# A two-layer decoder trunk on one core: the last products cut into columns of 512, 256 and 256, the last row normalised in other steps, and new tables of orders

## The chip, the cores and the metric

One Trainium2 chip; the program runs on one of its cores. Five engines work side by side, each through its own list of instructions: TensorE (PE, matmuls; PEld are its weight loads), VectorE (DVE), ScalarE (ACT), GpSimd (POOL) and SyncE (SP, which here only starts transfers). They wait for one another through semaphores. The metric is the device time of one execution in microseconds (us); lower is better. Before the change three runs gave 552.26, 552.55 and 552.84 us.

## What is computed

Two layers over 256 positions of width 1024, all in float32. Each layer has a token mixer (gated spatial mixing in the first, causal attention in the second) beside cross-attention into 256 memory tokens, one output projection, and a SwiGLU channel mixer. Each of the two sublayers ends in a residual and a layer norm:

```python
sub = jnp.concatenate([mix, mem_out], axis=-1) @ w_mix_out[i]
x = layer_norm(ALPHA * x + sub, ln_mix_g[i], ln_mix_b[i])
x = layer_norm(ALPHA * x + swiglu(x, w_ffn_in[i], w_ffn_out[i]), ln_ffn_g[i], ln_ffn_b[i])
```

The change is in the second of these norms in the last layer, whose result is the output.

## The kernel before

The 256 positions are two row tiles of 128 partitions (tt = 0 and 1; `xres[tt]` holds the residual, 128 x 1024). Every operand of a product is split into a high part, which ScalarE rounds (L379), and a low part, the rest, which VectorE subtracts (L380); each product is then three matmuls (high by high, and the two mixed ones). Weights stream from HBM by SyncE into four raw buffers, are split into ten buffers `spl`, and are used once.

The first stage multiplies the input (`x0T`, transposed) with the weights `v` in eight slices of 128 rows, two slices to a transfer block `raw_v`; then come `hqm`, six products `pu`, `hkm` (memory keys, weights `km0`), `pvm` (memory values, `vm0`) and so on. The channel mixer has eleven chunks of 256 hidden columns, whose products go into the accumulators `fof` in the first layer and `fog` in the second.

The end: for tile 0 the last chunks are added to its accumulators, the residual is formed in two halves (L493, sums for mean and variance at L499), and `finish` normalises and stores it. For tile 1 (`last_tile`), the chunks before the last three are already in the accumulators and are added first (L896); the last three chunks, six terms of 128 rows by three passes, are multiplied in pieces of columns (`LAST_PIECES`: 512, 384, 128), each piece into a PSUM tile `last` of its own by 18 matmuls. After each piece VectorE adds it to the residual (L903) and takes its sums (L499), and at the end `finish` runs for tile 1. `finish` (L502 to L514) aggregates mean and variance `mv` (L505), adds epsilon (L507, on VectorE), raises the result to -0.5 on GpSimd (L508), giving the scale `rs`; then, piece by piece, it subtracts the mean and multiplies by the gain (L511), multiplies by `rs` and adds the offset (L512), and starts the transfer to the output (L514, the last piece by ScalarE's queue, the others by SyncE's). L511 needs only the mean, L512 also the scale.

What sets the order: PE's instructions run as the program is written. For VectorE, ScalarE and SyncE three tables of numbers (`VECTOR_ORDER`, `SCALAR_ORDER`, `SYNC_ORDER`) say in which order the instructions of the engine, counted as written, are put into its list; `keep_order` ties each to the one ahead of it, so that an engine never overtakes a waiting instruction. GpSimd's few instructions are placed by the scheduler.

Of the kernel before, what the change touches and what calls it, by code (L numbers as in the profile page):

```python
# [21 lines left out]
P = 128  # L22
D = 1024
# [6 lines left out]
PIECES = ((0, 512), (512, 1024))  # L30
LAST_PIECES = ((0, 512), (512, 896), (896, 1024))
# [7 lines left out]
EPS = 1e-5  # L39
# [154 lines left out]
class Stream:  # L194
# [128 lines left out]
)  # L323
SCALAR_ORDER = (
# [42 lines left out]
def build(nc, tc, ins, out):  # L367
    ET = mybir.EngineType
    with (
# [115 lines left out]
        class LayerNorm:  # L485
# [16 lines left out]
            def finish(self, gb, store=False):  # L502
                r, tt = self.r, self.tt
# [719 lines left out]
```

## Time and profile before

| | before |
|---|---|
| runs, median (lowest to highest) | 552.55 us (552.26 to 552.84) |
| span of the profiled execution, first to last instruction | 550.8 us |
| clock granted to TensorE, mean | 0.996 |
| HBM read, written | 119.42 MB, 1.05 MB |

The span is that of one execution, taken by the hardware profiler; the runs are timed from outside, and their median lies 1.75 us above the span. In a timeline row stand the start in us from the span's beginning, the duration, the engine, the line, the operation, output and inputs, shapes, the count, and in brackets the idle time of the engine ahead of it and what ended it. In a row of the chain of work that ended last stand start, duration, engine, tile, line and count.

### The profile page before, as it was taken

To read this page: it belongs to the slowest core of one execution; us is meant where nothing else is said; L and a number is where in the kernel's file an instruction comes from. 1 tells how busy PE (TensorE), PEld (TensorE's weight loads), DVE (VectorE), ACT (ScalarE), POOL (GpSimd) and SP (SyncE) were. 2 spreads that over 40 slices of the span, in tenths; PEclk is the share of its full clock that TensorE was granted. 3 is DMA by queue.
4 is the path that set the end of the run, shared out by engine and by line. 5 is a ranking of instruction groups with operands and counts; after the bars stand their busy time and mean duration, and the time that the engine had idled before them with its cause. 6 is when DMAs were issued, how large, how long until landed. Compare 5 with 4: busy or idle time off the path is not lost.

```text
span 550.8 us, 7698 instructions
## 1 busy us (share of the span) xinstructions
PE 542.6 (99%) x2835; PEld 460.6 (84%) x2835; DVE 501.5 (91%) x707; ACT 374.5 (68%) x574; POOL 47.7 (9%) x59
## 2 busy tenths in 40 slices
PE   9999999999999999999999999999999999999994
PEld 8988878888888888888898888788888888888884
DVE  5799978999999999999989688589999999999997
ACT  5868759785858677683565667668768676876720
POOL 1012001020202020100000000111202020201000
PEclk9999999999999999999999999999999999999998
DMA  8997668479796988878539234513597698897622
GB/s 303 384 398 265 223 259 221 154 131 328 155 343 132 300 220 229 275 271 273 198 137 397 105 130 161 114 77 153 97 360 133 249 266 271 233 255 220 218 69 77
DMA packets 23718, 120.97 MB, mean 220 GB/s; under 512 B 2688, under 2 KB 4736, under 8 KB 13824
## 3 DMA queue, kind: packets, MB, share of 16 engines
q1 hardware_dynamic: 17344, 99.16, 47.8%
q0 software_dynamic: 5760, 20.97, 21.4%
q8 instruction: 22, 0.36, 0.3%
q10 hardware_dynamic: 576, 0.34, 0.3%
q14 instruction: 16, 0.13, 0.1%
HBM read 119.42 MB, written 1.05 MB: 219 GB/s over the span
## 4 chain that ended last, share of the span: by engine, by line
PE 98%; DMA 1%; DVE 1%; DVEq 0%; ACT 0%; issue 0%
PE fof L404 11%; PE Xf L404 10%; PE Xg L404 10%; PE fog L404 9%; PE Zg L404 7%; PE Zf L404 7%; PE qk L404 6%; PE opc L404 4%; PE opa L404 4%; PE va L404 3%; PE bv L404 3%; PE pu L404 3%; PE pvm L404 3%; PE hkm L404 2%; PE hqm L404 2%; PE pg L404 2%
## 5 line engine op out<-in xcount | busy, mean ns | idle before, releaser
L379 ACT CAST spl_s_M<-raw_s_T 128x1024 fp32r<-128x1024 f32 x80 | 82.4, 1052 | 22.9 <-DVE raw_s_T L259 18.0
L380 DVE TENSOR_TENSOR spl_s_M<-raw_s_T,spl_s_M 128x1024 fp32r<-128x1024 f32 x80 | 95.6, 1217 | 2.4 <-ACT spl_s_M L379 2.1
L380 DVE TENSOR_TENSOR spl_s_M<-raw_s,spl_s_M 128x1024 fp32r<-128x1024 f32 x60 | 71.7, 1217 | 3.2 <-ACT spl_s_M L379 3.1
L379 ACT CAST spl_s_M<-raw_s 128x1024 fp32r<-128x1024 f32 x60 | 61.0, 1050 | 17.5 <-DMA raw_s<-in_w 13.3
L404 PE MATMUL fof<-spl_w,htf 128*128 128x512 f32 x264 | 63.0, 390 | 0.0
L404 PEld LDWEIGHTS fof<-spl_w,htf 128*128 128x128 f32 x264 | 49.3, 188 | 10.2
L404 PE MATMUL fog<-spl_w,htg 128*128 128x512 f32 x228 | 54.2, 390 | 0.0
L380 DVE TENSOR_TENSOR spl_w<-raw_w,spl_w 128x1024 fp32r<-128x1024 f32 x44 | 53.2, 1215 | 0.1
L404 PEld LDWEIGHTS fog<-spl_w,htg 128*128 128x128 f32 x228 | 42.7, 188 | 8.8
L259 DVE TENSOR_TENSOR raw_s_T<-raw_s_T,raw_s 128x1024 f32<-128x1024 f32 x40 | 48.4, 1217 | 0.1
L379 ACT CAST spl_w<-raw_w 128x1024 fp32r<-128x1024 f32 x44 | 45.7, 1055 | 1.0 <-PE fof L404 1.0
L404 PE MATMUL qk<-x2T,spl_qk 128*128 128x512 f32 x192 | 36.0, 343 | 0.0
L220 POOL DMA_DIRECT2D raw_s<-in_w x20 | 17.1, 856 | 217.1 <-DVE spl_s_M L380 201.4
L404 PEld LDWEIGHTS qk<-x2T,spl_qk 128*128 128x128 f32 x192 | 29.4, 188 | 4.4
L404 PE MATMUL Xg<-spl_s_M,SgM 128*128 128x512 f32 x120 | 29.4, 394 | 0.0
L404 PE MATMUL Xf<-spl_s_M,SfM 128*128 128x512 f32 x120 | 29.3, 393 | 0.0
L404 PE MATMUL Zg<-spl_s_M,SgM 128*128 128x512 f32 x120 | 28.9, 390 | 0.0
L404 PE MATMUL Xf<-spl_s_M,x1T 128*128 128x512 f32 x120 | 28.9, 390 | 0.0
L404 PE MATMUL Zf<-spl_s_M,SfM 128*128 128x512 f32 x120 | 28.8, 389 | 0.0
L404 PE MATMUL Xg<-spl_s_M,x3T 128*128 128x512 f32 x120 | 28.8, 389 | 0.0
L404 PEld LDWEIGHTS Zg<-spl_s_M,SgM 128*128 128x128 f32 x120 | 22.5, 188 | 4.8 <-DVE SgM L380 0.2
L404 PEld LDWEIGHTS Xg<-spl_s_M,x3T 128*128 128x128 f32 x120 | 22.5, 188 | 4.7
(265 smaller groups left out, 1068.8 us busy)
## 6 DMA issues: line engine op xcount, KB each, us to landing
raw_w<-in_w SPq DMA_DIRECT2D x22, 1024.0 KB, 6.6
raw_s<-in_w SPq DMA_DIRECT2D x20, 1024.0 KB, 7.1
raw_s_T<-in_w SPq DMA_DIRECT2D x10, 1024.0 KB, 7.0
raw_s_T<-in_w POOLq DMA_DIRECT2D x20, 512.0 KB, 8.6
raw_s<-in_w POOLq DMA_DIRECT2D x20, 512.0 KB, 5.5
raw_o<-in_w SPq DMA_DIRECT2D x8, 1024.0 KB, 6.4
raw_qk<-in_w SPq DMA_DIRECT2D x6, 1024.0 KB, 4.8
raw_v<-in_w SPq DMA_DIRECT2D x7, 512.0 KB, 8.1
```

Source lines behind the costliest of these rows:

```text
L220: self.nc.gpsimd.dma_start(self.raw[name][:, sl], self.unit_ap(other)[:, sl], accum_op=ALU.add)
L259: self.nc.vector.tensor_add(raw, raw, self.raw[used[1]][:, sl])
L379: nc.scalar.copy(hi, src)
L380: nc.vector.tensor_sub(lo, src, hi.bitcast(F32))
L404: nc.tensor.matmul(o, lhsT, rhs, start=start, stop=stop, skip_group_check=on)
```

## The change

`LAST_PIECES` becomes 512, 256, 256. In `finish`, tile 1 now adds epsilon on GpSimd, subtracts the mean in one step of 1024 columns and scales in two steps of 768 and 256 columns, stored by SyncE and ScalarE; tile 0 goes from three pieces to two of 512, both stored by SyncE. The program's numbering changes with it, and all three tables are replaced as a whole.

```diff
-LAST_PIECES = ((0, 512), (512, 896), (896, 1024))
+LAST_PIECES = ((0, 512), (512, 768), (768, 1024))
+END_PIECES = ((0, 768), (768, 1024))
...
 VECTOR_ORDER = (
-    0, 2, 3, 4, 5, 6, 7, 8, 9, 10, 11, 12, 13, 14, 16, 15, 18, 17, 19, 20, 22, 21, 23, 24, 34, 29, 33, 25, 32, 38, 37,
+    0, 2, 4, 3, 6, 5, 7, 8, 10, 11, 9, 12, 14, 13, 15, 16, 18, 19, 17, 20, 22, 21, 23, 24, 31, 29, 33, 34, 1, 55, 37,
...
                 rs = sm(f"rs{self.nm}{tt}")
-                nc.vector.tensor_scalar_add(rs, mv[:, 1:2], EPS)
+                last = store and tt == 1
+                (nc.gpsimd if last else nc.vector).tensor_scalar_add(rs, mv[:, 1:2], EPS)
                 nc.gpsimd.tensor_tensor(rs, rs, mhalf, ALU.pow)
-                for i, (c0, c1) in enumerate(LAST_PIECES if store else PIECES):
+                for c0, c1 in ((0, D),) if last else PIECES:
                     sl = slice(c0, c1)
                     nc.vector.scalar_tensor_tensor(r[:, sl], r[:, sl], mv[:, 0:1], gb[:, 0, sl], ALU.subtract, ALU.mult)
+                for i, (c0, c1) in enumerate(END_PIECES if last else PIECES):
+                    sl = slice(c0, c1)
                     nc.vector.scalar_tensor_tensor(r[:, sl], r[:, sl], rs, gb[:, 1, sl], ALU.mult, ALU.add)
                     if store:
-                        (nc.scalar if i == len(LAST_PIECES) - 1 else nc.sync).dma_start(out[tt * P:(tt + 1) * P, sl], r[:, sl])
+                        (nc.scalar if last and i else nc.sync).dma_start(out[tt * P:(tt + 1) * P, sl], r[:, sl])
```

Four lines of the file are added ahead of and in this function, so a line of the old numbering stands 1 to 4 lines lower in the new one (L380 is L381, L512 is L516, L903 is L907).

What the change puts where is shown at three places of VectorE's list. The first is the end of the program, from the add of the last piece on. Before:

```order
L903 TENSOR_TENSOR xres<-xres,last_4984 128x128
L499 BN_STATS stg_4939<-xres 128x6
L505 BN_AGGR mvg_5005<-stg_4939 128x2
L511 SCALAR_TENSOR_TENSOR xres<-xres,mvg_5005,gb1ffn 128x128
L507 TENSOR_SCALAR rsg_5007<-mvg_5005 128x1
L511 SCALAR_TENSOR_TENSOR xres<-xres,mvg_5005,gb1ffn 128x384
L511 SCALAR_TENSOR_TENSOR xres<-xres,mvg_5005,gb1ffn 128x512
L512 SCALAR_TENSOR_TENSOR xres<-xres,rsg_5007,gb1ffn 128x128
L512 SCALAR_TENSOR_TENSOR xres<-xres,rsg_5007,gb1ffn 128x384
L512 SCALAR_TENSOR_TENSOR xres<-xres,rsg_5007,gb1ffn 128x512
```

The same place now, with the last scale of tile 0 (`rsg_4927`) ahead of it:

```order
L516 SCALAR_TENSOR_TENSOR xres<-xres,rsg_4927,gb1ffn 128x512
L907 TENSOR_TENSOR xres<-xres,last_4981 128x256
L500 BN_STATS stg_4936<-xres 128x6
L506 BN_AGGR mvg_5002<-stg_4936 128x2
L513 SCALAR_TENSOR_TENSOR xres<-xres,mvg_5002,gb1ffn 128x1024
L516 SCALAR_TENSOR_TENSOR xres<-xres,rsg_5004,gb1ffn 128x768
L516 SCALAR_TENSOR_TENSOR xres<-xres,rsg_5004,gb1ffn 128x256
```

Ten steps became six; epsilon left VectorE and stands on GpSimd ahead of the power there, and the smallest scale, which came first, now comes last.

The second place is the start of the first stage on VectorE: the cast of a slice of `x0T`, its low part, and the low parts of the weight slices (`spl_v0_0` is the first, `spl_v0_1` the second; both halves of the first transfer block `raw_v0`). Before:

```order
L439 CAST x0T_80<-raw_v0_135 128x256
L440 TENSOR_TENSOR x0T_80<-raw_v0_135,x0T_80 128x256
L380 TENSOR_TENSOR spl_v0_0_136<-raw_v0_135,spl_v0_0_136 128x384 x2
L439 CAST x0T_80<-raw_v0_135 128x256
L440 TENSOR_TENSOR x0T_80<-raw_v0_135,x0T_80 128x256
L380 TENSOR_TENSOR spl_v0_1_158<-raw_v0_135,spl_v0_1_158 128x384 x2
```

Now:

```order
L440 CAST x0T_80<-raw_v0_135 128x256
L381 TENSOR_TENSOR spl_v0_0_136<-raw_v0_135,spl_v0_0_136 128x384
L441 TENSOR_TENSOR x0T_80<-raw_v0_135,x0T_80 128x256
L440 CAST x0T_80<-raw_v0_135 128x256
L381 TENSOR_TENSOR spl_v0_0_136<-raw_v0_135,spl_v0_0_136 128x384
L441 TENSOR_TENSOR x0T_80<-raw_v0_135,x0T_80 128x256
L381 TENSOR_TENSOR spl_v0_1_158<-raw_v0_135,spl_v0_1_158 128x384
```

The second low part of the first slice moved behind the cast of the second slice.

The third place is VectorE's stretch ahead of `hkm`, with the low part of the second half of `km0` (`spl_km0_1`). Before:

```order
L965 SCALAR_TENSOR_TENSOR vn_318<-vn_318,mvv0_581,gv_308 128x768
L380 TENSOR_TENSOR memT2_525<-mraw2_314,memT2_525 128x512
L961 BN_AGGR mvv1_588<-stv1_366 128x2
L380 TENSOR_TENSOR spl_km0_1_545<-raw_km0_305,spl_km0_1_545 128x1024
L951 TENSOR_TENSOR uT1_423<-uT1_423,pu11_451 128x256
```

Now:

```order
L970 SCALAR_TENSOR_TENSOR vn_318<-vn_318,rsv0_583,gv_308 128x768
L965 BN_AGGR mvv1_588<-stv1_366 128x2
L955 TENSOR_TENSOR uT1_423<-uT1_423,pu11_451 128x256
L967 TENSOR_SCALAR rsv1_590<-mvv1_588 128x1
L381 TENSOR_TENSOR spl_vm0_0_603<-raw_vm0_391,spl_vm0_0_603 128x1024
L969 SCALAR_TENSOR_TENSOR vn_318<-vn_318,mvv1_588,gv_308 128x768
L381 TENSOR_TENSOR spl_vm0_1_614<-raw_vm0_391,spl_vm0_1_614 128x1024
L381 TENSOR_TENSOR spl_km0_1_545<-raw_km0_305,spl_km0_1_545 128x1024
```

The step moved behind one add of `uT1`, two steps of `vn` and both low parts of `vm0`.

112 rows, old and new, of tables (SCALAR_ORDER, SYNC_ORDER, VECTOR_ORDER) are left out of this document.

## The prediction, made before the changed kernel ran

> **What bounds the kernel now.** I read the page first (busy shares and the clock), then PE's waits, then the chain of work that ended last, then the timeline of the last 16 us.
>
> ```profile
> span 550.8 us, 7698 instructions
> PE 542.6 (99%) x2835; PEld 460.6 (84%) x2835; DVE 501.5 (91%) x707; ACT 374.5 (68%) x574; POOL 47.7 (9%) x59
> PE 98%; DMA 1%; DVE 1%; DVEq 0%; ACT 0%; issue 0%
> PE warmup L415 <- DVE warm L410: 1.1, 1, 1.1
> ```
>
> The first two lines are totals: TensorE (PE) is busy in 99% of the span. The third is the chain that ended last, 98% of it PE. The fourth is the only row in which the list of waits names PE itself as waiting. So the time can change in three ways only: PE gets less work, PE begins to wait, or the stretches before its first and behind its last matmul change.
>
> All durations come from the one profiled execution, with a span of 550.8 us. The median of the runs is 552.55, so 1.75 us lie outside the span; I make the sum against 550.8 and add the same 1.75.
>
> ```profile
> 242.17 2.72 PE Zf L404 x12
> 279.45 9.36 PE bv L404 x54
> 288.81 5.55 PE hqm L404 x32
> 534.57 9.26 PE last L404 x54
> ```
>
> These rows of the chain give the pitch of back-to-back matmuls. 512 columns: 2.72/12 = 0.227 us. 384 columns: 9.36/54 = 0.173. hqm alternates 512 and 256 columns: 5.55/16 = 0.347 a pair, less 0.227 is 0.120 for 256. The last products are 18 of each width, so 128 columns cost (9.26 - 18 x 0.227 - 18 x 0.173)/18 = 0.114, hardly less than 256.
>
> **The last products.** 18 x (0.227 + 0.120 + 0.120) = 8.41 instead of 9.26: **-0.85 us**, all on the bounding engine.
>
> This is where a rule of the Trainium skill speaks against the change: "TensorE: Matmul & The Clock Gate", Back-to-back issue gap, puts a warm matmul at N/2.4 + 2.5 ns, so that 384 + 128 columns cost as much as 256 + 256. By it this term would be nil. The measured 0.114 for 128 columns is twice its 0.056, so I go by the rows.
>
> **Behind the last matmul.** It ends at 534.57 + 9.26 = 543.83; call that E.
>
> ```profile
> 535.35 0.68 DVE L499 BATCH_NORM_STATS2 stg<-xres 128x6 f32<-128x512 f32 x1
> 543.85 0.29 DVE L903 TENSOR_TENSOR xres<-xres,last 128x128 f32<-128x128 f32 x1
> 544.17 0.29 DVE L499 BATCH_NORM_STATS2 stg<-xres 128x6 f32<-128x128 f32 x1
> 544.50 0.24 DVE L505 BATCH_NORM_AGGREGATE mvg<-stg 128x2 f32<-128x18 f32 x1
> 544.77 0.35 DVE L511 SCALAR_TENSOR_TENSOR xres<-xres,mvg,gb1ffn 128x128 f32<-128x128 f32 x1
> 545.04 0.15 DVE L507 TENSOR_SCALAR rsg<-mvg 128x1 f32<-128x1 f32 x1
> 545.11 0.61 DVE L511 SCALAR_TENSOR_TENSOR xres<-xres,mvg,gb1ffn 128x384 f32<-128x384 f32 x1
> 545.27 0.85 POOL L508 TENSOR_TENSOR rsg<-rsg,mhalf 128x1 f32<-128x1 f32 x1 [7.93 <-DVE rsg L507]
> 545.63 0.74 DVE L511 SCALAR_TENSOR_TENSOR xres<-xres,mvg,gb1ffn 128x512 f32<-128x512 f32 x1
> 547.09 0.74 DVE L512 SCALAR_TENSOR_TENSOR xres<-xres,rsg,gb1ffn 128x512 f32<-128x512 f32 x1
> 51.08 0.41 DVE L951 TENSOR_TENSOR uT<-uT,pu 128x256 f32<-128x256 f32 x1
> 51.60 1.02 DVE L966 SCALAR_TENSOR_TENSOR vn<-vn,rsv,gv 128x768 f32<-128x768 f32 x1
> ```
>
> Columns: start, duration, engine, line, instruction. Before, the power on POOL lay beside the subtractions, and DVE never waited: its last step ends at 547.83 = E + 4.00. Now:
>
> - the add and the sums take 256 columns instead of 128: 0.41 (the uT row is an add from PSUM of that width) and about 0.43 (between 0.29 for 128 and 0.68 for 512). With 0.03 between steps and the aggregate's 0.24, the mean is ready at E + 1.19 instead of E + 0.91.
> - one subtraction of 1024 columns. From 0.35 for 128 and 0.74 for 512 follows 1.0 ns a column, so 1.27: E + 1.22 to E + 2.50.
> - beside it POOL now has two steps, epsilon and power. Epsilon on POOL is nowhere in the trace, and what matters is whether POOL may start.
>
> ```profile
> 374.87 1.22 DVE L380 TENSOR_TENSOR spl_s_M<-raw_s_T,spl_s_M 128x1024 fp32r<-128x1024 f32 x1
> 375.04 1.46 POOL L522 TENSOR_TENSOR rsc<-rsc,mhalf 128x1 f32<-128x1 f32 x1 [9.82 <-DVE rsc L521]
> 80.71 0.55 POOL L522 TENSOR_TENSOR rsa<-rsa,mhalf 128x1 f32<-128x1 f32 x1 [29.14 <-DVE rsa L521]
> 80.77 1.23 DVE L380 TENSOR_TENSOR spl_s_M<-raw_s_T,spl_s_M 128x1024 fp32r<-128x1024 f32 x1
> 91.03 0.41 DVE L470 TENSOR_TENSOR kkm<-hkm,kkm 128x256 fp32r<-128x256 f32 x1
> 91.21 0.56 POOL L522 TENSOR_TENSOR rsa<-rsa,mhalf 128x1 f32<-128x1 f32 x1 [3.93 <-DVE rsa L521]
> ```
>
> The same power of 128 x 1 takes 0.55 when it starts ahead of the DVE step (80.71) or beside one that reads PSUM (91.03), and 1.46 when a DVE step with two SBUF operands already runs: it then ends 0.41 behind that step (376.09, 376.50). At 545.27 too: DVE's 384-column step ended at about 545.72, the power at 546.12. The new epsilon waits for the aggregate, as the subtraction does; POOL started 0.08 behind its releaser in the last power, DVE 0.03. So I take it that DVE is first and POOL is held until E + 2.50; then epsilon 0.41, power 0.42, 0.03 to DVE: the scale is there at E + 3.36. DVE, which had this cover before, now **stands idle 0.9 us**. Bounds for the two POOL steps: if nothing holds them and both take the 0.55 of a free power, the scale is ready at E + 2.4, before the subtraction ends; if epsilon costs as much as the slowest power here, 1.46, it comes 1.05 later.
>
> The Trainium skill ("SBUF — State Buffer", SBUF: two separate sides) says that whichever of the two starts first holds the shared ports for its whole instruction. Were POOL first, DVE's subtraction would wait some 0.5 us and the power would queue behind it, about 0.2 us later than my sum. That half isn't seen here: at 80.77 DVE took its usual 1.23 beside a running power.
>
> - the 768-column scale: 1.02 (the vn row): E + 4.38, against E + 4.00 for the last step before. The 256-column one ends at about E + 4.78.
>
> ```profile
> out<-xres SPq DMA_DIRECT2D x2, 256.0 KB, 2.2
> out<-xres SPq DMA_DIRECT2D x2, 192.0 KB, 1.9
> out<-xres ACTq DMA_DIRECT2D x2, 64.0 KB, 1.6
> ```
>
> The last column is issue to landing. 0.3 for each 128 KB more: 384 KB takes 2.35 to 2.8, I take 2.5, that is 0.3 more than the 256 KB that ended the kernel. The 128 KB from ACT (about 1.75) is issued 0.4 later and lands first. So the end moves to **E + 0.38 + 0.30 = 0.68 later behind E**.
>
> Whether DVE is ready at the new E: the first tile's last scale (0.74) stands just ahead of the last add. The pieces now end at 538.7, 540.8 and 542.98. Between 540.8 and 542.98 DVE has an add (0.41), two sums (0.68 and 0.43) and that scale (0.74): 2.26, less the 0.08 by which steps overlap, 2.0. It fits with nothing to spare; no term.
>
> **The start.**
>
> ```profile
> 5.31 17.52 PE va L404 x96
> 5.29 1.07 DVE L380 TENSOR_TENSOR spl_v<-raw_v,spl_v 128x384 fp32r<-128x384 f32 x2
> 7.17 0.29 DVE L439 CAST x0T<-raw_v 128x256 fp32r<-128x256 f32 x1 [0.80 <-DMA raw_v<-in_w]
> 7.42 0.85 PE L404 MATMUL va<-spl_v,x0T 128*128 128x384 f32 x4
> ```
>
> PE needs the second low part of the first weight slice at its eleventh matmul, two behind the 7.42 at which the fourth row begins: 7.42 + 2 x 0.173 = 7.77. Before, it was ready at 6.36. In the new DVE order it stands behind the cast that waits for a DMA until 7.17: 7.17 + 0.29 + 0.55 = 8.01. PE has run without a gap since, so the **0.24 us** stay to the end. No later load lets PE regain it.
>
> **The rest of the tables.** PE's order is the same but for the last 54 matmuls. The step that lost most room is the low part of km0's second half.
>
> ```profile
> 37.86 1.16 DVE L380 TENSOR_TENSOR spl_km<-raw_km,spl_km 128x1024 fp32r<-128x1024 f32 x1
> 45.02 5.55 PE hkm L404 x32
> 30.00:38.00 8.00, 8.00 (x48) 7.06 (x48) 8.00 (x15) 5.22 (x8) 0.00 (x0) 1.00 1.00 411
> ```
>
> The third row is a stretch of 8 us with the busy time of PE, weight loads, DVE, ACT and POOL. The step ended at 39.02, and PE uses it from its ninth matmul on, 45.02 + 4 x 0.347 = 46.41. Ahead of it now stand two adds (0.41 each), two steps of 768 (1.02), two low parts of vm0 (about 1.2) and small ones: 5.6 us, so 44.6 if nothing else is late. 1.8 us of room are left of 7.4. At the other places where I set the work now ahead of a step against the time at which PE needs it, some tenths of a microsecond or more remain; I cost those moves at nothing, covered by the work that PE still has in hand there, with 0 to 1 us as bounds.
>
> **Sum:** -0.85 + 0.68 + 0.24 = +0.07: 550.9 of span, **552.6 us**.
>
> **Rivals.**
>
> 1. POOL isn't held by the subtraction (the epsilon gets through as the power at 80.71 did). For it: only some 0.05 us separate the two starts. Against it: the row at 375.04. DVE's idle 0.9 goes: 551.7, and 551.2 if the 384 KB land as fast as 256 KB and the start keeps its room.
> 2. Slower: DVE reaches km0's second half late. Place: PE at 46.4. It decides once DVE is more than 1.8 us behind; beyond that each microsecond costs one. For it: DVE is busy 8.00 of the 8.00 us between 30 and 38, and in the new ScalarE order two activations that wait for PE's last va matmul (22.83) stand ahead of the casts of u0. With 3.5 us of delay: 552.6 + 1.7 = 554.3.
> 3. 256 columns save nothing over 384 + 128, as the formula has it: the -0.85 falls out, 553.5. Against it: 0.120 is measured in 16 pairs of hqm.
>
> **How the numbers follow.** My forecast, POOL held, no new wait beyond the start, 551.9 to 553.4 with its DMA and epsilon bounds: 0.56. Rival 1: 0.22. Rival 2: 0.17. Rival 3: 0.05. About 0.2%, 1.1 us, is what a measurement of this kernel can tell from no change; so faster is below 551.45, slower above 553.65. Faster: about half of rival 1, 0.11. Slower: rival 2, and a little of the forecast's upper end and of rival 3: 0.19. Same: 0.70. The range runs from rival 1 with a short start to rival 2 at 1.4 us beyond the forecast: 551.3 to 554.0.
>
> **What would show it.** The chain's last-products piece at 8.4 us; POOL's epsilon ending about 0.4 behind the end of the 1024-column subtraction and DVE idle some 0.9 us before the 768-column scale; last DVE step to span end near 3 us; va at 17.7 to 17.8 instead of 17.52. I am wrong on POOL if epsilon ends while the subtraction runs, and on the tables if PE shows a wait of more than 0.3 us anywhere behind the start.

## The result, and the profile after

| | before | after |
|---|---|---|
| runs, median (lowest to highest) | 552.75 us (552.26 to 553.15, 6 runs) | 555.24 us (554.39 to 557.17, 6 runs) |
| ratio after to before | | 1.0051 (95% interval 1.0039 to 1.0063) |
| span of the profiled execution | 550.8 us | 552.7 us |
| last matmul ends | 543.83 | 544.50 |
| from there to the end of the span | 6.97 | 8.20 |

The change made the kernel slower by 2.5 us; 552.6 was predicted, between 551.3 and 554.0. The profiled execution of the changed kernel took 554.39 us, the fastest of its six, so its trace shows the least of the loss, 1.9 us of span. First its totals and the whole list of waits of PE:

```profile
span 552.7 us, 7683 instructions
PE 542.6 (98%) x2835; PEld 459.4 (83%) x2835; DVE 500.4 (91%) x701; ACT 375.0 (68%) x574; POOL 50.4 (9%) x60
PE warmup L416 <- DVE warm L411: 1.0, 1, 1.0
PE hkm L405 <- DVE spl_km L381: 0.8, 1, 0.8
```

PE still bounds, but there is a second row where before had one: hkm waits for the low part of km0. The chain of work that ended last says where else the time went (start, duration, tile, line, count):

```profile
5.17 17.78 PE va L405 x96
34.14 3.03 PE pu L405 x16
47.85 4.34 PE hkm L405 x23
52.19 2.77 PE pvm L405 x16
536.03 8.47 PE last L405 x54
```

The stage va ends at 22.95 instead of 5.31 + 17.52 = 22.83 (+0.12). pvm begins at 52.19 instead of 45.02 + 5.55 = 50.57: +1.50 more, in the stretch in which the chain leaves PE between 37 and 47.85. The last products begin at 536.03 instead of 534.57, so 0.16 was regained in between. They take 8.47 instead of 9.26 (-0.79), and the stretch behind them is 8.20 instead of 6.97 (+1.23). 0.12 + 1.50 - 0.16 - 0.79 + 1.23 = 1.90, the whole of it.

The 1.50 is more than the one wait in the list. PE's and its weight loads' timelines, after and then (last row) before:

```profile
28.34 17.14 PE L405 MATMUL pu<-x0T,spl_u 128*128 128x512 f32 x96
47.85 4.34 PE L405 MATMUL hkm<-memT,spl_km 128*128 128x256 f32 x23 [0.76 <-DVE spl_km L381]
48.45 3.43 PEld L405 LDWEIGHTS hkm<-memT,spl_km 128*128 128x128 f32 x20 [0.19 <-DVE memT L381]
28.22 16.80 PE L404 MATMUL pu<-x0T,spl_u 128*128 128x512 f32 x96
```

The products pu took 0.34 longer, hkm waited 0.76 for km0, and the other 0.40 lie in what is left of hkm behind that wait, where the weight loads wait once more, for a part of memT that VectorE makes after km0's.

The stretch ahead of hkm, in the timeline of VectorE and GpSimd, after and then (last two rows) before:

```profile
42.02 1.22 DVE L381 TENSOR_TENSOR spl_vm<-raw_vm,spl_vm 128x1024 fp32r<-128x1024 f32 x1
43.16 1.01 DVE L969 SCALAR_TENSOR_TENSOR vn<-vn,mvv,gv 128x768 f32<-128x768 f32 x1
44.09 2.58 DVE L381 TENSOR_TENSOR spl_vm<-raw_vm,spl_vm 128x1024 fp32r<-128x1024 f32 x1
46.59 1.21 DVE L381 TENSOR_TENSOR spl_km<-raw_km,spl_km 128x1024 fp32r<-128x1024 f32 x1
43.62 1.97 POOL L933 TENSOR_SCALAR_AFFINE_SELECT wsT<-wsT 128x1536 f32<-128x1536 f32 x1
```

```profile
39.84 1.55 POOL L929 TENSOR_SCALAR_AFFINE_SELECT wsT<-wsT 128x1536 f32<-128x1536 f32 x1 [37.78 <-DMA wsT<-in_wsT]
40.87 1.60 DVE L380 TENSOR_TENSOR spl_vm<-raw_vm,spl_vm 128x1024 fp32r<-128x1024 f32 x1 [0.46 <-ACT spl_vm L379]
```

The reader is to see the 2.58: a step that takes 1.22 elsewhere ended 1.08 after GpSimd's select of wsT did (43.62 + 1.97 = 45.59). The select, which no table lists, was placed behind the second power `rsv` by the scheduler. The same is in the trace of before, in small: 1.60, ended 1.08 behind the select. The prediction had overlooked that row.

The end, in the timelines of VectorE and GpSimd, and the transfers from issue to landing:

```profile
544.52 0.42 DVE L907 TENSOR_TENSOR xres<-xres,last 128x256 f32<-128x256 f32 x1 [0.15 <-PE last L405]
544.98 0.43 DVE L500 BATCH_NORM_STATS2 stg<-xres 128x6 f32<-128x256 f32 x1
545.44 0.24 DVE L506 BATCH_NORM_AGGREGATE mvg<-stg 128x2 f32<-128x18 f32 x1
545.71 1.28 DVE L513 SCALAR_TENSOR_TENSOR xres<-xres,mvg,gb1ffn 128x1024 f32<-128x1024 f32 x1
547.77 1.41 DVE L516 SCALAR_TENSOR_TENSOR xres<-xres,rsg,gb1ffn 128x768 f32<-128x768 f32 x2 [0.77 <-POOL rsg L510]
545.77 1.32 POOL L509 TENSOR_SCALAR rsg<-mvg 128x1 f32<-128x1 f32 x1 [5.96 <-DVE mvg L506]
547.17 0.57 POOL L510 TENSOR_TENSOR rsg<-rsg,mhalf 128x1 f32<-128x1 f32 x1
out<-xres SPq DMA_DIRECT2D x1, 384.0 KB, 2.4
out<-xres ACTq DMA_DIRECT2D x1, 128.0 KB, 2.4
```

Epsilon took 1.32 because the subtraction held it, and VectorE stood idle for 0.77. VectorE's last step ends at 549.18, 4.68 behind the last matmul (before 4.00), and from there to the end it is 3.52 (before 2.97): ScalarE's 128 KB took 2.4 us, as long as the 384 KB of the other queue, and ended the kernel.

### The profile page after: what moved, and what is told of

It reads as the page before. It is cut to its first block, busy times and chain, and to the rows that moved or that the text cites. A ratio compares the mean times of both kernels' runs of the same rounds, so it can differ in the third digit from the quotient of the medians.

```text
span 552.7 us, 7683 instructions
## 1 busy us (share of the span) xinstructions
PE 542.6 (98%) x2835; PEld 459.4 (83%) x2835; DVE 500.4 (91%) x701; ACT 375.0 (68%) x574; POOL 50.4 (9%) x60
## 4 chain that ended last, share of the span: by engine, by line
PE 96%; DVE 2%; ACT 0%; POOL 0%; issue 0%; POOLq 0%; DVEq 0%
PE fof L405 11%; PE Xg L405 10%; PE Xf L405 10%; PE fog L405 9%; PE Zg L405 7%; PE Zf L405 7%; PE qk L405 6%; PE opc L405 4%; PE opa L405 4%; PE va L405 3%; PE bv L405 3%; PE pvm L405 3%; PE hqm L405 2%; PE pg L405 2%; PE pf L405 2%; PE hkm L405 2%
## 5 line engine op out<-in xcount | busy, mean ns | idle before, releaser
L380 ACT CAST spl_s_M<-raw_s_T 128x1024 fp32r<-128x1024 f32 x80 | 82.5, 1051 | 24.9 <-DVE raw_s_T L260 14.0
L381 DVE TENSOR_TENSOR spl_s_M<-raw_s_T,spl_s_M 128x1024 fp32r<-128x1024 f32 x80 | 95.5, 1217 | 2.0 <-ACT spl_s_M L380 1.9
L381 DVE TENSOR_TENSOR spl_s_M<-raw_s,spl_s_M 128x1024 fp32r<-128x1024 f32 x60 | 71.7, 1216 | 2.3 <-ACT spl_s_M L380 2.3
L380 ACT CAST spl_s_M<-raw_s 128x1024 fp32r<-128x1024 f32 x60 | 61.0, 1050 | 14.8 <-DMA raw_s<-in_w 13.3
L405 PE MATMUL fof<-spl_w,htf 128*128 128x512 f32 x264 | 63.0, 390 | 0.0
L405 PEld LDWEIGHTS fof<-spl_w,htf 128*128 128x128 f32 x264 | 49.3, 188 | 10.2
L405 PE MATMUL fog<-spl_w,htg 128*128 128x512 f32 x228 | 54.2, 390 | 0.0
L381 DVE TENSOR_TENSOR spl_w<-raw_w,spl_w 128x1024 fp32r<-128x1024 f32 x44 | 53.1, 1217 | 0.2 <-ACT spl_w L380 0.2
L405 PEld LDWEIGHTS fog<-spl_w,htg 128*128 128x128 f32 x228 | 42.7, 188 | 8.8
L380 ACT CAST spl_w<-raw_w 128x1024 fp32r<-128x1024 f32 x44 | 45.9, 1051 | 1.3 <-ACT spl_w L380 0.8
L405 PE MATMUL qk<-x2T,spl_qk 128*128 128x512 f32 x192 | 36.0, 343 | 0.0
L405 PEld LDWEIGHTS qk<-x2T,spl_qk 128*128 128x128 f32 x192 | 29.4, 188 | 4.4
L405 PE MATMUL Xf<-spl_s_M,SfM 128*128 128x512 f32 x120 | 29.4, 393 | 0.0
L405 PE MATMUL Xg<-spl_s_M,SgM 128*128 128x512 f32 x120 | 29.4, 393 | 0.0
L405 PE MATMUL Xg<-spl_s_M,x3T 128*128 128x512 f32 x120 | 29.1, 390 | 0.0
L405 PE MATMUL Xf<-spl_s_M,x1T 128*128 128x512 f32 x120 | 28.9, 389 | 0.0
L405 PE MATMUL Zf<-spl_s_M,SfM 128*128 128x512 f32 x120 | 28.8, 389 | 0.0
L405 PE MATMUL Zg<-spl_s_M,SgM 128*128 128x512 f32 x120 | 28.8, 389 | 0.0
L221 POOL DMA_DIRECT2D raw_s_T<-in_w x20 | 17.5, 877 | 121.9 <-DVE mix L381 69.7
L405 PEld LDWEIGHTS Xg<-spl_s_M,x3T 128*128 128x128 f32 x120 | 22.4, 188 | 5.0 <-DVE x3T L381 0.4
```

The source lines that it names most:

```text
L221: self.nc.gpsimd.dma_start(self.raw[name][:, sl], self.unit_ap(other)[:, sl], accum_op=ALU.add)
L380: nc.scalar.copy(hi, src)
L381: nc.vector.tensor_sub(lo, src, hi.bitcast(F32))
L405: nc.tensor.matmul(o, lhsT, rhs, start=start, stop=stop, skip_group_check=on)
```

## The experiments

Three theories stood against each other. Theory 1: the loss ahead of the last products is the wait at hkm, made by the select. Theory 2: it belongs to the tables as a whole, at several places. Theory 3: it belongs to the changed end. Each was timed beside runs of the kernel before on the same chip, in groups on five chips; whether the chip adds to the spread between versions isn't shown. "new" and "old" are the tables after and before, the old ones with the numbers of the new program.

| version | ratio to before (interval) | profiled span |
|---|---|---|
| again: after, once more | 1.0060 (1.0047 to 1.0073) | 552.6 |
| end_alone: old tables, new end | 1.0005 (0.9997 to 1.0014) | 551.0 |
| tables_alone: new tables, old end | 1.0039 (1.0027 to 1.0051) | 552.5 |
| no_select | 1.0037 (1.0023 to 1.0050) | 552.1 |
| km_first | 1.0052 (1.0039 to 1.0064) | 555.1 |
| early_back: first 60 us old | 1.0017 (1.0005 to 1.0030) | 552.9 |
| late_back: first 60 us new | 1.0037 (1.0024 to 1.0051) | 552.4 |
| start_back: first 24 us old | 1.0031 (1.0019 to 1.0043) | 551.9 |
| last_v_first | 1.0028 (1.0014 to 1.0043) | 554.8 |
| engines_early | 1.0045 (1.0030 to 1.0061) | 553.7 |
| sync_early | 1.0168 (1.0147 to 1.0189) | 559.5 |
| late_v: before, one transfer late | 1.0042 (1.0030 to 1.0055) | 553.3 |
| m5g_first | 1.0039 (1.0026 to 1.0052) | 552.7 |
| out_halves | 1.0033 (1.0021 to 1.0045) | 553.6 |
| eps_vector | 1.0020 (1.0010 to 1.0031) | 553.0 |
| columns_alone | 0.9993 (0.9984 to 1.0001) | 551.1 |
| columns_again | 0.9994 (0.9985 to 1.0002) | 550.3 |
| small_last | 1.0003 (0.9994 to 1.0011) | 550.4 |

**Tables or end.** The changed kernel again, and each half of the change alone. end_alone takes the old order up to the first instruction of the changed end; tables_alone is the kernel of before with the new order up to there (651, 535 and 112 numbers), the old one behind it. The diff is in short form: OLD and NEW stand for the lists of numbers.

```diff
-VECTOR_ORDER = NEW
+VECTOR_ORDER = OLD[:658] + [i for i in NEW if i not in OLD[:658]]
...
-SCALAR_ORDER = NEW
+SCALAR_ORDER = OLD[:535] + [i for i in NEW if i not in OLD[:535]]
...
-SYNC_ORDER = NEW
+SYNC_ORDER = OLD[:112] + [i for i in NEW if i not in OLD[:112]]
```

> The changed kernel as it is, for a second profile and as the measure of the three runs beside it. Its median was 2.5 us above before, the one profiled execution 1.9. If the early waits of PE hang on the order alone, this profile shows them again: a wait of about 0.9 us in hkm at 46.7 with the VectorE step of vm0 ahead of it stretched to 2.6 us, and 0.25 us at 34.1. If they were an accident of that execution, hkm follows pu without a wait and the spread of the runs is the cause.

> The changed end (columns 512, 256, 256, epsilon on GpSimd, one subtraction, two scales) with the old tables up to the end of the program. If the tables cost what stands ahead of the last products (1.46 us in the profile), only the end is left: -0.8 for the last products, +1.2 behind the last matmul, so 0.4 us above before, ratio 1.0005 to 1.001, and no wait of PE in hkm. If the end carries the loss, the ratio is that of the changed kernel, 1.004 to 1.005.

> The new tables with the old end (columns 512, 384, 128 and the old steps). If the tables carry the loss ahead of the end: 1.5 us above before in the profile, 1.5 to 2.1 in the median, ratio 1.003 to 1.004, with the wait of about 0.9 us in hkm and the stretched VectorE step. If the loss belongs to the end, ratio 1.000.

The two halves came out as expected, 1.0005 and 1.0039. Theory 3 falls; by these ratios the end costs some 0.3 us and the tables some 2. But the second profile of the same changed kernel loses its time elsewhere. PE's and ScalarE's timelines there, with ScalarE's row before for the cast of the same last slice at the bottom:

```profile
6.14 14.85 PE L405 MATMUL va<-spl_v,x0T 128*128 128x384 f32 x84 [0.31 <-DVE x0T L441]
21.65 2.03 PE L405 MATMUL va<-spl_v,x0T 128*128 128x384 f32 x10 [0.67 <-DVE x0T L441]
19.13 0.41 ACT L440 CAST x0T<-raw_v 128x256 fp32r<-128x256 f32 x1 [3.42 <-DMA raw_v<-in_w]
15.88 0.40 ACT L439 CAST x0T<-raw_v 128x256 fp32r<-128x256 f32 x1
```

va waits 0.67 us for the last slice of the input, whose transfer ScalarE awaited until 19.13 (18.41 in the first profile). Before, that transfer was issued at 5.6 and landed 10.2 later, at 15.8, and ScalarE's cast at 15.88 did not wait. hkm had no wait in this execution, though the select stretched the same step to 2.57, because PE came to it 0.40 later and VectorE 0.77 earlier. tables_alone showed the third form of that collision:

```profile
43.67 1.21 DVE L380 TENSOR_TENSOR spl_vm<-raw_vm,spl_vm 128x1024 fp32r<-128x1024 f32 x1
43.20 4.84 POOL L929 TENSOR_SCALAR_AFFINE_SELECT wsT<-wsT 128x1536 f32<-128x1536 f32 x1
```

Here VectorE's step took its usual time and the select was held, for 4.84 us, though it began 0.47 us ahead of that step in this execution as in the first (43.62 and 44.09). It was so in eps_vector too, again 4.84; in five other profiles of the new early lists (again, late_back, last_v_first, out_halves and km_first) the select got in and VectorE's step behind it took 2.57. What decides which of the two waits isn't shown.

**The wait at hkm.** no_select leaves the select out; km_first exchanges two steps of VectorE.

```diff
-        nc.gpsimd.affine_select(
-            out=wsT, in_=wsT, compare_op=ALU.is_ge, fill=0.0, base=0,
-            pattern=[[0, 12], [1, P]], channel_multiplier=-1)
```

```diff
-    46, 56, 45, 41, 32, 25, 26, 38, 27, 35, 42, 57, 49, 39, 47, 28, 30, 58, 59, 40, 60, 63, 61, 64, 50, 48, 44, 43, 62,
+    46, 56, 45, 41, 32, 25, 26, 38, 27, 35, 42, 57, 49, 39, 47, 28, 30, 58, 59, 40, 60, 63, 61, 50, 64, 48, 44, 43, 62,
```

> The changed kernel without the affine select on GpSimd that blanks the upper triangle of wsT, so the first layer's spatial mixing is computed unmasked. Theory 1: the select, started at 43.62 ahead of the second low part of vm0, keeps VectorE from its SBUF operands until 45.59; without it that step takes 1.22 instead of 2.58, the low part of km0's second half ends near 46.4 instead of 47.8, PE (which needs it at 46.9) waits less than 0.1 us in hkm, and the time falls by 0.9 to 1.1 us against the changed kernel. Theory 2: VectorE's list is simply too long ahead of that step, whatever GpSimd does; then the step stays at 2.6 us or another fills the place, PE waits about 0.9 us as before, and the time stays.

> The changed kernel, with two steps of VectorE's list exchanged: the low part of km0's second half stands ahead of the second low part of vm0. If that place costs what no_select gave back (1.3 us of the median), the same comes back without touching GpSimd: ratio 1.0035 to 1.0045, and no wait of PE at hkm, since the step now ends by 46.7 even where it is the one that the select holds back. If the place costs time in few executions only, nothing: 1.005 to 1.006.

```profile
43.90 1.22 DVE L381 TENSOR_TENSOR spl_vm<-raw_vm,spl_vm 128x1024 fp32r<-128x1024 f32 x1
```

This row of no_select shows the mechanism: without the select the step takes 1.22, and hkm didn't wait. As a share of the loss it is uncertain: 1.0037 against 1.0051 and 1.0060, and km_first gave nothing back (1.0052). Its profiled execution, 556.8 us, shows why one place is not the answer:

```profile
PE pu L405 <- DVE qqm L478: 0.8, 1, 0.8
PE hkm L405 <- DVE memT L381: 0.7, 1, 0.7
PE tpg L834 <- DVE m5g L813: 0.6, 1, 0.6
PE va L405 <- DVE spl_v L381: 0.4, 1, 0.4
PE va L405 <- DVE x0T L441: 0.3, 1, 0.3
PE Zf L405 <- ACT Zf L807: 0.2, 1, 0.2
```

Six waits of PE at five products, where the kernel before has none behind its start. The 0.3 at va for x0T is no sign of the new lists: in columns_alone, with the old ones, PE waits there twice, 0.6 in all. Theory 1 falls as the whole cause.

**Which stretch of the tables.** The first 60 us in the old order, the reverse of that, and the first 24 us in the old order.

```diff
-VECTOR_ORDER = NEW
+VECTOR_ORDER = OLD[:79] + [i for i in NEW if i not in OLD[:79]]
...
-SCALAR_ORDER = NEW
+SCALAR_ORDER = OLD[:67] + [i for i in NEW if i not in OLD[:67]]
...
-SYNC_ORDER = NEW
+SYNC_ORDER = OLD[:31] + [i for i in NEW if i not in OLD[:31]]
```

(For start_back the numbers are 25, 25 and 19. In late_back OLD and NEW change places, with 76, 63 and 31.)

> The changed kernel, but what VectorE, ScalarE and SyncE begin in the first 60 us stands in the old order; the rest as in the new tables. The end costs +0.4 us against before in every version of it. Theory A, the new tables lose their time in the first 60 us (the first stage and hkm): 553.2 to 553.6, ratio 1.001 to 1.0015. Theory B, they lose it at several places that have become thin, the products tpg near 413 us among them, where the last two profiles showed a wait of 0.4 and 0.9 us on VectorE: 553.8 to 554.5, ratio 1.002 to 1.003, with a wait of PE at tpg in the profile.

> The other way round: the new order in the first 60 us, the old one behind it, the changed end. Theory A: as the changed kernel, ratio 1.005 to 1.006. Theory B: about 1.003 to 1.004, and no wait at tpg near 413 us, while va or hkm wait.

> The changed kernel with only the first 24 us in the old order (the stage va). By the profiles the start of va to its end lost 0.1 to 0.85 us from execution to execution with the new order (hqm began at 22.8, 23.5, 23.1, 23.0 instead of 22.7). If that is its share, ratio 1.0035 to 1.0045, with hqm at 22.3 to 23.0. If the whole loss of the first 60 us (1.0017 against 1.0055) lies here, 1.0015 to 1.002; if none, 1.005 to 1.006.

1.0017, 1.0037 and 1.0031 lie between end_alone and the changed kernel: no stretch alone seems to carry the loss, which fits Theory 2. It is weak evidence, since versions with equal lists differ as much (see The end). What is left in early_back stands in its list of waits; with it ScalarE's timeline ahead of that place, GpSimd's row for the first of four transfers that it issues there, and the same row before:

```profile
PE tpg L834 <- DVE m5g L813: 0.9, 1, 0.9
408.17 2.00 ACT L380 CAST spl_s_M<-raw_s_T 128x1024 fp32r<-128x1024 f32 x2 [3.16 <-DMA raw_s_T<-in_w]
392.55 0.89 POOL L221 DMA_DIRECT2D raw_s<-in_w  x1 [15.76 <-ACT m5g L773]
389.88 0.87 POOL L220 DMA_DIRECT2D raw_s<-in_w  x1 [13.38 <-ACT spl_s_M L379]
```

GpSimd issues the four transfers of raw_s and raw_s_T from 392.55 on instead of 389.88, ScalarE then waits 3.16 us for the last, VectorE gets late to m5g, and PE waits 0.9 us at tpg. The late first issue is not the whole of it: the last of the four was issued at 397.52, as before (397.59), but landed 10.6 instead of 6.2 us later; why isn't shown. m5g_first is early_back with m5g moved ahead of two steps:

```diff
-    529, 530, 533, 535, 528, 534, 536, 537, 538, 540, 531, 541, 532, 542, 543, 551, 539, 553, 544, 545, 547, 548, 546,
+    529, 530, 528, 533, 535, 534, 536, 537, 538, 540, 531, 541, 532, 542, 543, 551, 539, 553, 544, 545, 547, 548, 546,
```

> As early_back (old order in the first 60 us, ratio 1.0017), and on VectorE the product m5g ahead of the two additions of weight blocks that stand before it near 411 us. With the wait of PE at tpg gone (0.9 us in that profile): ratio 1.0005 to 1.001, no wait at tpg; that all of the tables' late loss is that one wait. If the late loss has other places (Zf near 242 us lost 0.55 to 0.7 in that profile), 1.001 to 1.0015.

Missed: 1.0039. The wait at tpg was gone, and PE waited at 420.57 instead, 6 us behind that place ("PE Xg L405 <- DVE htg L381: 0.4, 1, 0.4" in its list of waits). Here, with the data late, the order of the steps that use it only chose where PE notices.

**The transfers.** In SyncE's new list the last 512 KB of raw_v (number 8, the last slice) stand behind the two transfers of raw_qm (10 and 9), and those wait for a raw buffer to come free: number 8 was issued at 10.4 instead of 5.6 us. (Each slice is a transfer of its own, and two share a buffer; the 14.5 us in the expectations of last_v_first and late_v is where the slice ahead of this one landed.) last_v_first puts 8 back; sync_early puts SyncE's whole first 60 us back, engines_early those of VectorE and ScalarE (numbers as in early_back); late_v makes the one move in the kernel of before.

```diff
-    0, 1, 2, 3, 4, 5, 6, 7, 10, 9, 8, 11, 13, 18, 12, 19, 20, 14, 21, 15, 17, 16, 24, 22, 25, 23, 26, 27, 28, 29, 33,
+    0, 1, 2, 3, 4, 5, 6, 7, 8, 10, 9, 11, 13, 18, 12, 19, 20, 14, 21, 15, 17, 16, 24, 22, 25, 23, 26, 27, 28, 29, 33,
```

```diff
-    0, 1, 2, 3, 4, 18, 5, 6, 7, 8, 10, 9, 11, 12, 13, 14, 15, 19, 20, 16, 17, 24, 22, 25, 21, 26, 27, 28, 29, 23, 31,
+    0, 1, 2, 3, 4, 18, 5, 6, 7, 10, 9, 8, 11, 12, 13, 14, 15, 19, 20, 16, 17, 24, 22, 25, 21, 26, 27, 28, 29, 23, 31,
```

> The changed kernel with one transfer put back in SyncE's list: the last 512 KB of raw_v ahead of the two of raw_qm. It is then issued near 5.2 instead of 10.4 us and lands near 14.5 instead of 18.4. If PE's waits in the second half of va (0.8 us at 20.65 in one profile) and the lateness behind them come from it: ratio 1.0035 to 1.0045 instead of 1.0055, hqm at 22.5 to 22.9. If not: 1.005 to 1.006.

> The changed kernel with SyncE's whole list of the first 60 us put back, VectorE's and ScalarE's as changed. If the order of the transfers carries the early loss: 1.0015 to 1.0025, as early_back. If the two engines' lists carry it: 1.0045 to 1.006.

> The other half: VectorE's and ScalarE's first 60 us in the old order, SyncE's as changed. If the order of the transfers carries the early loss: 1.0045 to 1.006, since the old lists now wait for transfers that come later. If the two engines' lists carry it: 1.0015 to 1.0025.

> The kernel of before with one transfer moved in SyncE's list: the last 512 KB of raw_v behind the two of raw_qm, as the new table has it. Theory: it lands near 18 instead of 14.5 us, PE waits in the last slices of va (0.5 to 1.2 us near 20.5) and what follows is late: ratio 1.002 to 1.003. Rival: the stage has room for it with the old lists, and the new lists are the cause: 0.9995 to 1.0005.

late_v is the clearest result of the study: one transfer moved in the kernel of before costs 2.1 us of the median, 1.0042, more than expected. Its timelines of PE and ScalarE:

```profile
22.04 0.62 PE L404 MATMUL va<-spl_v,x0T 128*128 128x384 f32 x2 [1.31 <-ACT spl_v L379]
23.37 2.02 PE L404 MATMUL va<-spl_v,x0T 128*128 128x384 f32 x10 [0.71 <-DVE x0T L440]
19.45 0.41 ACT L439 CAST x0T<-raw_v 128x256 fp32r<-128x256 f32 x1 [3.06 <-DMA raw_v<-in_w]
```

The transfer lands at 19.4 instead of 15.8, and PE waits 1.31 and 0.71 us for the last two slices; nothing later gives it back. In the new lists the same transfer is late too (18.41 and 19.13), and putting it first brought 1.0028, a difference that equal lists show as well. engines_early, the old lists with the new order of transfers, stayed at 1.0045, as late_v would have it. sync_early missed both expectations, at 1.0168, for a reason of its own:

```profile
42.21 0.62 ACT L380 CAST memT<-mraw 128x512 fp32r<-128x512 f32 x1 [7.75 <-DMA mraw<-in_memT]
44.55 7.44 PE L405 MATMUL pu<-x0T,spl_u 128*128 128x512 f32 x32 [4.67 <-DVE uT L955]
```

SyncE's old list sends the last memory tokens late, ScalarE's new list wants them early and stood still for 7.75 us. SyncE's list and ScalarE's were one plan, and this mix broke it.

**The end.** out_halves and eps_vector are the changed kernel with one edit each; columns_alone (and columns_again) is the kernel of before with one edit; small_last is that with its last scales and transfers in another order.

```diff
-END_PIECES = ((0, 768), (768, 1024))
+END_PIECES = ((0, 512), (512, 1024))
```

```diff
-                (nc.gpsimd if last else nc.vector).tensor_scalar_add(rs, mv[:, 1:2], EPS)
+                nc.vector.tensor_scalar_add(rs, mv[:, 1:2], EPS)
```

```diff
-LAST_PIECES = ((0, 512), (512, 896), (896, 1024))
+LAST_PIECES = ((0, 512), (512, 768), (768, 1024))
```

```diff
-    661, 666, 663, 670, 664, 662, 671, 672, 673, 674, 675, 681, 676, 679, 677, 682, 680, 678,
+    661, 666, 663, 670, 664, 662, 671, 672, 673, 674, 675, 681, 676, 679, 677, 678, 682, 680,
...
-    113, 112, 115, 114,
...
+    114, 115,
```

> The changed kernel, with the last row scaled and sent in halves of 512 columns instead of 768 and 256. Theory: ScalarE's transfer of 128 KB began 1.42 us after its issue, and ended the kernel, because the 384 KB of SyncE's queue were still moving; alone it begins 0.86 after it. With 256 KB issued first, 0.27 us earlier, the queue is almost free when the second is due: stretch from the last matmul to the end 7.8 to 8.0 instead of 8.2 us. Rival: a transfer on ScalarE's queue behind one on SyncE's always begins 1.4 us after its issue, and now carries 256 KB: 8.3 to 8.5 us.

> The changed kernel with epsilon of the last row on VectorE, ahead of the one subtraction. Theory: the subtraction of 1024 columns holds GpSimd, so the power ends 0.41 us behind it, as behind the 1024-column step at 375; VectorE idles 0.45 instead of 0.77 us, pays 0.07 to 0.15 for epsilon, and the stretch behind the last matmul is 0.2 us shorter, 8.0. Rival: the power gets in ahead of the subtraction, no idle time, 7.5 us. The ratio moves by less than its interval: 1.0045 to 1.006.

> The kernel of before with the last pieces of 512, 256, 256 columns as its only edit (its own tables and its own finish, whose pieces then have those widths too). -0.79 us on PE as measured; behind it the last add and sums of 256 instead of 128 columns, +0.13 each; the subtractions and scales have the same columns in all: ratio 0.999, about -0.5 us. If the tail costs 1.2 us whatever the steps are, ratio 1.0007.

> The kernel of before with columns of 512, 256, 256 as its only edit, once more: 0.9993 came out (0.9984 to 1.0001), by its profile's terms -0.79 on PE and +0.44 behind the last matmul, so -0.35 us or 0.9994. The same again, or it was chance and the ratio is above 1.

> As the one beside it, and the piece of 512 columns is scaled and sent first, the two of 256 behind it (by ScalarE's and SyncE's queue), so that 128 KB and not 256 KB end the kernel. If a transfer costs its own issue to landing (1.6 us for 64 KB, 1.9 for 192, 2.2 for 256), another -0.3 to -0.4 us: ratio 0.9983. If the small transfers wait for the packets of the 256 KB ahead of them, as ScalarE's 128 KB did in the changed kernel behind 384 KB, nothing or -0.1 against the one beside it.

out_halves: 7.8 us behind the last matmul instead of 8.2, as the theory had it, and ScalarE's transfer, twice as large, landed sooner ("out<-xres ACTq DMA_DIRECT2D x1, 256.0 KB, 2.1"). eps_vector: GpSimd's and VectorE's rows,

```profile
546.57 1.52 POOL L510 TENSOR_TENSOR rsg<-rsg,mhalf 128x1 f32<-128x1 f32 x1 [6.14 <-DVE rsg L509]
548.13 1.41 DVE L516 SCALAR_TENSOR_TENSOR xres<-xres,rsg,gb1ffn 128x768 f32<-128x768 f32 x2 [0.44 <-POOL rsg L510]
```

show the power held to 0.41 behind the subtraction (546.41 + 1.27 = 547.68), 0.44 of idle time, and 7.9 us behind the last matmul. Its ratio of 1.0020 is lower than 0.27 us can explain: versions with the same lists up to the end came out between 1.0020 and 1.0060 here, so differences between versions of the new lists below some 0.004 are not evidence by themselves.

columns_alone and columns_again gave 0.9993 and 0.9994, each with an interval that reaches just above 1; taken together, with an interval narrower by the square root of 2, about 0.9988 to 0.9999. That is the fastest version found, by an estimated 0.4 us. small_last lost what it was to win: its 128 KB on ScalarE's queue were again issued behind a larger transfer of SyncE's and took 2.1 us instead of the 1.9 in columns_alone, where nothing stood ahead of them, and the stretch behind the last matmul was 7.7 us against 7.4.

## Why the prediction was wrong

- **The last products** (-0.85): right, -0.79 measured, 8.47 instead of 9.26, and rival 3 falls. The prediction set the Trainium skill's formula ("TensorE: Matmul & The Clock Gate", Back-to-back issue gap) against this term. That section gives the formula for an isolated matmul, and says itself that it is too low for narrow ones in a stream that loads weights; the 0.114 us for 128 columns, twice what the formula gives, agrees with the latter.
- **GpSimd held at the end**: right. Epsilon ended 0.1 instead of 0.41 behind the subtraction, the power took 0.57 instead of 0.42, VectorE idled 0.77 (0.9 predicted), and its last step ended 4.68 behind the last matmul (4.78 predicted). Rival 1 falls.
- **The output transfers** (+0.30): the mechanism was there, the size wrong. "The 128 KB from ACT (about 1.75) is issued 0.4 later and lands first" failed: it took 2.4 and landed last, so the stretch behind the last matmul grew by 1.23 instead of 0.68. On this queue 128 KB took 1.9 with nothing ahead (columns_alone), 2.1 behind 256 KB of SyncE's (small_last) and 2.4 behind 384. The Trainium skill ("DMA: Bandwidth & Descriptors", Queues, rings and completion order) says that each DMA engine alternates between queues only after a whole packet of several descriptors. The 2.4 would fit that; how many descriptors a packet held here isn't shown.
- **The start** (+0.24): va did take 17.78 (17.7 to 17.8 predicted), but by luck. The second low part, which PE was to await until 8.01, was ready at 6.95 + 0.56 = 7.51, ahead of the 7.77 at which it is needed, because the data had landed earlier (the cast began at 6.74, not 7.17):

```profile
6.95 0.56 DVE L381 TENSOR_TENSOR spl_v<-raw_v,spl_v 128x384 fp32r<-128x384 f32 x1
```

va also began 0.14 earlier than before, so that it ended only 0.12 later. The wait that was priced does show in other executions, with 0.4 in km_first. And the step looked at VectorE's list and not at SyncE's: the late raw_v transfer was passed over, and it is worth up to 0.67 us in the one profile and 2.1 us of the median in the kernel of before.

- **"At the other places ... I cost those moves at nothing"**: this is the step that failed. Ahead of the last products the new order cost 1.34 us in the fastest execution (1.46 less the start's 0.12; pu and hkm took 0.34 and 1.16 longer, and 0.16 was regained), and the tables cost some 2 us in the median of tables_alone, against a bound of 1. At hkm the prediction had seen 1.8 us of room, "if nothing else is late"; other things were. The sign that it had named for being wrong on the tables, a wait of more than 0.3 us behind the start, came with the 0.76 at hkm. What the runs showed in its place: transfers land later in the new order (the last of raw_v at 18.4 to 19.1 instead of 15.8, the last of raw_s_T at 408 instead of 404), the lists have lost their room at va, pu, hkm, Zf and tpg, and which of these places costs, and how much, changes from execution to execution.
- **Rival 2** had the place, hkm near 46.4, and the sign, and came nearest to the time (554.3). Its mechanism (ScalarE's activations delay VectorE) is a part of what the trace shows. The low part of km0's second half ended at 46.59 + 1.21 = 47.80 instead of the 44.6 of the prediction. 1.36 of these 3.2 us came from GpSimd's select, which it had not counted; the other 1.8 had used up the room by then. ScalarE did wait for va and cast u0 2.25 us later than before (first two rows; the third is before), and VectorE idled for such casts (last row; 0.72 and 0.29 ahead of it):

```profile
22.82 0.87 ACT L945 ACTIVATE vn<-va 128x384 f32<-128x384 f32 x2 [1.36 <-PE va L405]
23.57 1.05 ACT L380 CAST spl_u<-raw_u 128x1024 fp32r<-128x1024 f32 x1
21.32 1.99 ACT L379 CAST spl_u<-raw_u 128x1024 fp32r<-128x1024 f32 x2
30.98 1.23 DVE L381 TENSOR_TENSOR spl_u<-raw_u,spl_u 128x1024 fp32r<-128x1024 f32 x1 [0.60 <-ACT spl_u L380]
```

How much of the 1.8 is ScalarE's isn't shown: it also waited for transfers of raw_u. The rule quoted from the Trainium skill ("SBUF — State Buffer", SBUF: two separate sides), that whichever starts first holds the shared ports for its whole instruction, agrees with both traces (VectorE's 1.60 and 2.58 behind a running select), and the prediction's "That half isn't seen here" was wrong. In tables_alone and eps_vector it doesn't tell the outcome: the select had the earlier start and was held.

Shown: the end costs 0.44 us by the trace (1.23 - 0.79; end_alone's ratio allows -0.2 to 0.8), the tables the rest; the late transfer costs 2.1 us in the old lists; the select stretches a step by 1.36. Open: how the new lists' 2 us are shared between the late transfer, hkm and the places behind 240 us. The versions that undo one of them differ by less than versions with equal lists do.

## What to carry to other kernels

Where a list of transfers is reordered, set each transfer's landing against the first use of its data, and look at what it now stands behind: a transfer that waits for a buffer holds all behind it. Lists that were planned together have their slack together; count the places that have become thin, because each is paid in some of the executions, and removing one wait may only move it, as in m5g_first, if the data is late. Price an instruction that the table doesn't list, such as GpSimd's, where it may fall, not where it fell before.

## What the runs showed of the hardware

- GpSimd's select and VectorE's steps with two SBUF operands shut each other out for whole instructions, either way: VectorE's step took 2.58 instead of 1.22, or the select 4.84 instead of 1.55.
- A transfer on ScalarE's queue took 2.4 us for 128 KB behind 384 KB of SyncE's queue, 2.1 us for 256 KB behind 256 KB issued 0.67 earlier, and 1.9 us for 128 KB with nothing ahead.
- One transfer of 512 KB that landed 3.6 us later than before (19.4 instead of 15.8) cost a kernel in which TensorE is busy in 99% of the span 2.1 us.
